# First products of a feed-forward by seven block products in place of eight

## The chip, the cores and the metric

The kernel runs on one core of a Trainium2 chip. Its time is the device time of one execution in microseconds (us); the figure for a kernel is the median of several executions. One execution of each kernel is also taken by the hardware profiler, and from that come the pages and rows shown here. TensorE is called PE there (PEld its weight load), VectorE DVE, ScalarE ACT, GpSimd POOL, and SyncE, which issues the loads, SP.

## The reference, cut to what matters

Two layers work on 512 latent tokens and, up to the end of the first layer, also on 256 context tokens. A layer is a half-step SwiGLU feed-forward, a mixer of four groups of heads, and a second feed-forward:

```python
def swiglu(h, w_in, w_out):
    u = h @ w_in                                    # 1024 x 5632
    return (jax.nn.silu(u[..., :D_FF]) * u[..., D_FF:]) @ w_out   # D_FF = 2816
...
x = x + 0.5 * mod[:, 2] * swiglu(modulate(rms_norm(x, norm_g[l, 0]), mod[:, 0], mod[:, 1]), ffn_w_in[l, 0], ffn_w_out[l, 0])
```

`modulate` scales and shifts each of the 1024 features; scale, shift and gate come from a product of a conditioning vector with `w_mod`, one set for the latent tokens and one for the context. The whole is in float32.

## The kernel before, in words

The stream xT lies in SBUF, features on partitions: eight tiles (KT) of 128 features by 768 tokens (T), the 512 latent tokens first and then the 256 of the context. Each weight and each activation of a large product is split in two fp32r parts, a high one (ScalarE rounds it) and a low one (VectorE subtracts; `split`, L371), and a product is three matmuls: high by high, high weight by low, low weight by high (`mm3`, L361). PE is given new weights for each matmul.

There are four feed-forward passes (`ffn`, L381): two in each layer. The last has the 512 latent tokens only. A pass runs over 22 blocks (`ff`) of 128 hidden features. For a block, the gate columns and the up columns of `ffn_w_in` are loaded as one raw tile of 128 x 2048 (w1r, L391), split as a whole, and multiplied over the eight feature tiles (u = 0 gate, u = 1 up) for both segments of tokens, 512 and 256 columns. Two more columns beside the second segment are the shifts of the modulation, so that their product gives the bias of the block (ub). The results in PSUM are scaled per token with the RMS norm (rsb) by VectorE (L419), ScalarE does SiLU, VectorE multiplies (L423), and the result is split again (gh, gl, L430 and L431). Blocks are gathered into chunks (CK, L1478); after the blocks of a chunk its second products run over the eight output tiles n_, and VectorE adds them to xT with the gate (L445). PSUM has seven banks for all of these.

In the background of the blocks, modulation vectors for later stages are made (`mod_block`, L201): tiles of `w_mod` of 1 MB are loaded and VectorE multiplies them by the conditioning vector and sums (macc, L213 and L215). Their instructions get a later place in the order (LATER).

Before a pass, `ready` (L335) is called after each finished tile of xT: it adds the tile's squares (`sumsq`) and makes its scaled high and low parts (`raw_tile`, L320) in hh and hlo. The last pass instead normalizes all tiles after the mixer (`norm_mod`, L344). The very first pass makes its own in a prologue (`first_mods`, L906), beside two modulation blocks on TensorE (`mod_direct`, L181).

The order on each engine is that of the program by these priorities, as a scheduler fixes it before the run; a dependence makes an engine wait, and then everything behind it on that engine waits. All loads are issued by SP, in order; a load waits until the tile that it overwrites is free.

## Time and profile before

| | |
|---|---|
| median of 3 runs | 3506.7 us (3506.53 to 3507.1) |
| the profiled execution | 3515.57 us, span 3513.8 us |
| PE busy | 3370.4 us, 96% of the span |
| DVE busy | 2001.4 us, 57% |
| ACT busy | 1144.4 us, 33% |
| POOL busy | 166.5 us, 5% |
| loaded from memory | 260.68 MB |

Busy time is the time in which an engine had an instruction at work; matmuls are pipelined and overlap, so a busy TensorE can still wait for short moments. The passes lie at 46 to 634, 1346 to 1943, 1943 to 2513 and 3100 to 3500 us of the span; the mixers lie between the first and the second and between the third and the fourth.

### The profile page before, as it was taken

The numbers are of one execution on the slowest core, as the hardware profiler recorded it, in microseconds if no ns is written. First come the engines' busy times: TensorE is split into PE (matmuls) and PEld (weight loads), VectorE is DVE, ScalarE is ACT, GpSimd is POOL, SyncE is SP. The second block draws the span as 40 slices with busy tenths as digits, with TensorE's granted clock in tenths as the row PEclk, the third lists the DMA queues.
The fourth block names the chain that finished last, engine by engine and source line by source line (L and its number), as shares of the span: only waits on it lengthen the run. The fifth ranks groups of instructions, "written<-read, shape, count | busy, mean of one in ns | idle before, by whom it ended". The sixth has DMA issues, their size and how long they took to land.

```text
span 3513.8 us, 54921 instructions
## 1 busy us (share of the span) xinstructions
PE 3370.4 (96%) x22756; PEld 2735.3 (78%) x22756; DVE 2001.4 (57%) x4351; ACT 1144.4 (33%) x2173; POOL 166.5 (5%) x350
## 2 busy tenths in 40 slices
PE   6999999999988999999999999999999989989997
PEld 5888888878666767888888788888888766667776
DVE  5776664555567856654445765443555568753333
ACT  3221122323456723211213112211333567532222
POOL 0000000000022310000000000000000022200000
PEclk8999999999999999999999999999999989999999
DMA  7444331211100014332121443331212100043330
GB/s 236 126 132 132 108 102 53 59 37 49 31 3 2 12 34 142 104 108 72 61 61 54 139 143 98 95 120 37 64 49 55 31 3 11 26 123 102 92 100 24
DMA packets 324121, 266.33 MB, mean 76 GB/s; under 512 B 27396, under 2 KB 273312, under 8 KB 323872
## 3 DMA queue, kind: packets, MB, share of 16 engines
q1 hardware_dynamic: 323872, 262.82, 24.5%
q8 instruction: 179, 2.93, 0.4%
q14 instruction: 70, 0.57, 0.1%
HBM read 260.68 MB, written 2.10 MB: 75 GB/s over the span
## 4 chain that ended last, share of the span: by engine, by line
PE 84%; DVE 10%; ACT 3%; issue 1%; DMA 1%; POOL 1%; DVEq 0%; SPq 0%; ACTq 0%; POOLq 0%
PE ul L365 13%; PE ul L367 13%; PE ul L369 13%; PE y L369 6%; PE y L367 6%; PE y L365 6%; PE pj L365 4%; PE pj L369 4%; PE pj L367 4%; PE op L1273 3%; PE S L1018 1%; PE ch L782 1%; DVE w1l L378 1%; PE gram L653 1%; PE po L1018 1%
## 5 line engine op out<-in xcount | busy, mean ns | idle before, releaser
L365 PE MATMUL ul<-hh,w1h 128*128 128x512 f32 (+1 forms) x2464 | 692.9, 350 | 2.5 <-ACT hh L357 1.6
L367 PE MATMUL ul<-hl,w1h 128*128 128x512 f32 (+1 forms) x2464 | 693.3, 348 | 1.5 <-DVE hl L358 1.5
L369 PE MATMUL ul<-hh,w1l 128*128 128x512 f32 (+1 forms) x2464 | 688.5, 348 | 1.5 <-DVE w1l L378 1.5
L365 PEld LDWEIGHTS ul<-hh,w1h 128*128 128x128 f32 x2464 | 395.9, 190 | 76.3 <-issue 9.9
L367 PEld LDWEIGHTS ul<-hl,w1h 128*128 128x128 f32 x2464 | 396.6, 190 | 66.4 <-DVE hl L358 2.2
L369 PEld LDWEIGHTS ul<-hh,w1l 128*128 128x128 f32 x2464 | 393.6, 189 | 63.9 <-DVE w1l L378 2.3
L367 PE MATMUL y<-gl,w2h 128*128 128x512 f32 x1232 | 342.8, 347 | 4.4 <-DVE gl L431 4.1
L369 PE MATMUL y<-gh,w2l 128*128 128x512 f32 x1232 | 339.0, 346 | 5.7 <-DVE w2l L378 5.7
L365 PE MATMUL y<-gh,w2h 128*128 128x512 f32 (+1 forms) x1232 | 340.1, 347 | 0.6 <-ACT gh L430 0.4
L377 ACT ACTIVATE w1h<-w1r 128x2048 fp32r<-128x2048 f32 x88 | 168.7, 1917 | 490.0 <-PE ul L367 454.1
L215 DVE SCALAR_TENSOR_TENSOR macc<-wm,sc,macc 128x512 f32<-128x512 f32 x392 | 274.2, 745 | 76.6 <-DMA wm<-in_w_mod_dram 75.2
L445 DVE SCALAR_TENSOR_TENSOR xT<-y,gate,xT 128x512 f32<-128x512 f32 x336 | 199.2, 631 | 192.3 <-PE y L369 191.7
L377 ACT ACTIVATE w2h<-wo 128x512 fp32r<-128x512 f32 (+1 forms) x192 | 111.6, 594 | 544.5 <-PE y L367 340.1
L365 PE MATMUL pj<-hh,pwh 128*128 128x512 f32 (+2 forms) x864 | 251.1, 342 | 3.9 <-DVE qA L945 1.8
L369 PE MATMUL pj<-hh,pwl 128*128 128x512 f32 (+2 forms) x864 | 243.0, 336 | 2.4 <-DVE pwl L378 2.4
L419 DVE TENSOR_TENSOR u<-ul,rsb 128x512 f32<-128x512 f32 (+1 forms) x132 | 70.8, 551 | 304.2 <-PE ul L369 304.2
L367 PE MATMUL pj<-hl,pwh 128*128 128x512 f32 (+2 forms) x864 | 242.9, 336 | 0.0
L369 PEld LDWEIGHTS y<-gh,w2l 128*128 128x128 f32 x1232 | 194.8, 188 | 40.0 <-DVE w2l L378 9.9
L367 PEld LDWEIGHTS y<-gl,w2h 128*128 128x128 f32 x1232 | 195.3, 188 | 38.3 <-DVE gl L431 8.9
L365 PEld LDWEIGHTS y<-gh,w2h 128*128 128x128 f32 x1232 | 195.4, 188 | 37.2 <-ACT w2h L377 3.1
L378 DVE TENSOR_TENSOR w1l<-w1r,w1h 128x2048 fp32r<-128x2048 f32 x88 | 201.2, 2286 | 26.6 <-ACT w1h L377 26.6
L421 ACT ACTIVATE sg<-sg,ub 128x512 f32<-128x512 f32 (+1 forms) x132 | 74.1, 609 | 425.7 <-DVE ub L416 321.0
(355 smaller groups left out, 4489.5 us busy)
## 6 DMA issues: line engine op xcount, KB each, us to landing
w1r<-in_ffn_w_in_dram SPq DMA_DIRECT2D x176, 512.0 KB
wm<-in_w_mod_dram SPq DMA_DIRECT2D x72, 1024.0 KB
wo<-in_ffn_w_out_dram SPq DMA_DIRECT2D x88, 512.0 KB
pw<-in_w_in_dram SPq DMA_DIRECT2D x46, 512.0 KB
pw<-in_w_in_dram SPq DMA_DIRECT2D x16, 256.0 KB
wo<-in_w_out_dram SPq DMA_DIRECT2D x128, 32.0 KB
wo<-in_w_out_dram SPq DMA_DIRECT2D x64, 64.0 KB
xl<-in_x_dram SPq DMA_DIRECT2D x4, 512.0 KB
```

The costliest lines, as they stand in the source:

```text
L215: nc.vector.scalar_tensor_tensor(out=acc[v], in0=r[:, k, :], scalar=s, in1=acc[v], op0=ALU.mult, op1=ALU.add)
L365: nc.tensor.matmul(p, lhsT=wh, rhs=xh[:, o:o + n], start=first, stop=False)
L367: nc.tensor.matmul(p, lhsT=wh, rhs=xl[:, o:o + n], start=False, stop=False)
L369: nc.tensor.matmul(p, lhsT=wl, rhs=xh[:, o:o + n], start=False, stop=last)
L377: nc.scalar.activation(out=hi, in_=raw, func=AF.Copy)
L378: nc.vector.tensor_tensor(out=lo, in0=raw, in1=hi, op=ALU.subtract)
L419: nc.vector.tensor_tensor(out=dst[:, o:o + n], in0=p, in1=self.rsb[:, o:o + n], op=ALU.mult)
L421: nc.scalar.activation(out=dst[:, o:o + n], in_=dst[:, o:o + n], func=AF.Silu, bias=b[:, u, s:s + 1])
L445: nc.vector.scalar_tensor_tensor(out=xs, in0=py[s], scalar=gt[s][:, n_:n_ + 1], in1=xs, op0=ALU.mult, op1=ALU.add)
L653: nc.tensor.matmul(pt[:, c, w], lhsT=BK[:, c, :], rhs=AR[:, e, c, w], start=True, stop=True)
L1018: mm = lambda out, lt, r, st, sp: nc.tensor.matmul(out, lhsT=lt, rhs=r, start=st, stop=sp, skip_group_check=True)
L1273: nc.tensor.matmul(p, lhsT=wt[:, i, :], rhs=os[i][:, osegs[i][v][0]:osegs[i][v][0] + c], start=i == 0, stop=i == m - 1)
```

## The change

The gate and up columns of a block, the even and the odd feature tiles, and the first and the second half of the tokens (H: 384 of 768, or 256 of 512) make a product of 2 x 2 by 2 x 2 blocks. It is done with seven block products in place of eight. `w1_operands` loads the four blocks of weights as tiles of 128 x 512 and makes four sums of them on GpSimd; each of the seven operands is split by itself, with four buffers for the parts. `up` issues the seven products, each 12 matmuls over 4 tiles, into three PSUM banks (b, c, a); ScalarE copies three partial results out, VectorE adds them to later ones, and results are also gathered in PSUM. The operands of the activations, B[0..6], are made for pairs of tiles when xT becomes ready (`pair_even`, `pair_odd`), two of the sums on GpSimd; the shift columns go with the four operands of SHIFTED.

Then the scaling by rsb is done by VectorE for one quarter of the results and by GpSimd for three. `up` of the next block, also across the end of a chunk, is issued behind the evaluation of a block and before the chunk's second products. The chunks become eight of two and three blocks. Tiles of `w_mod` are now 256 KB with two buffers, in the background and in the prologue, and the sums macc have one buffer each. The prologue loads the first block's weights once more to make its bias (bias0). `norm_mod` is gone; the last pass is prepared by `ready` as the others are. Before and after the feed-forwards that a mixer follows or precedes, the tiles hh and hlo and the tiles B take each other's place (`switch`).

```diff
+NWQ, NW1, NPC = 6, 4, 4
+MODPOOL = 0
+EVEN1, T1, T2, ODD1, T3, ODD2, T4 = range(7)
+SHIFTED = (EVEN1, T2, ODD1, T4)
...
+        acc = [self.fw.tile([128, 512], F32, name=f"macc{v}", tag=f"macc{v}", bufs=1) for v in vs]
+        for k in range(KT):
+            r = self.raw.tile([128, 512], F32, name="wm", tag="wm", bufs=2)
+            nc.sync.dma_start(out=r, in_=a["w_mod"][l, k * 128:(k + 1) * 128, b * 128:b * 128 + 512])
+                if k == 0:
+                    eng.tensor_scalar(out=acc[v], in0=r, scalar1=s, scalar2=None, op0=ALU.mult)
+                else:
+                    eng.scalar_tensor_tensor(out=acc[v], in0=r, scalar=s, in1=acc[v], op0=ALU.mult, op1=ALU.add)
         self.macc = l, b, vs, acc
...
+    def parts(self, i, m, x, scale=None):
+        nc = self.nc
+        hi, lo = (t[:, m, 2:] if i in SHIFTED else t[:, m, :] for t in self.B[i])
+        if scale is None:
+            nc.scalar.activation(out=hi, in_=x, func=AF.Copy)
+            nc.vector.tensor_tensor(out=lo, in0=x, in1=hi, op=ALU.subtract)
+        else:
+            nc.scalar.activation(out=hi, in_=x, func=AF.Copy, scale=scale)
+            nc.vector.scalar_tensor_tensor(out=lo, in0=x, scalar=scale, in1=hi, op0=ALU.mult, op1=ALU.subtract)
+    def second(self, k, segs, out):
+        H = self.half
+        for v, (o, n) in enumerate(segs):
+            o0, o1 = max(o, H), o + n
+            if o0 < o1:
+                self.nc.scalar.activation(out=out[:, o0 - H:o1 - H], in_=self.xT[k][:, o0:o1], func=AF.Copy, scale=self.rg[v][:, k:k + 1])
+    def pair_even(self, m, segs, e2):
+        k = 2 * m
+        self.parts(EVEN1, m, self.xT[k][:, :self.half], self.rg[0][:, k:k + 1])
+        self.second(k, segs, e2)
+    def pair_odd(self, m, segs, e2, o2, new):
+        nc, H = self.nc, self.half
+        e, o = self.xT[2 * m][:, :H], self.xT[2 * m + 1][:, :H]
+        ne, go = self.rg[-1][:, 2 * m:2 * m + 1], self.rg[0][:, 2 * m + 1:2 * m + 2]
+        self.second(2 * m + 1, segs, o2)
+        yield
+        t = new()
+        nc.vector.scalar_tensor_tensor(out=t, in0=e, scalar=ne, in1=e2, op0=ALU.mult, op1=ALU.add)
+        self.parts(T1, m, t)
+        yield
+        nc.gpsimd.tensor_tensor(out=t, in0=o2, in1=t, op=ALU.subtract)
+        self.parts(T2, m, t)
+        yield
+        self.parts(ODD1, m, o, go)
+        nc.gpsimd.tensor_tensor(out=e2, in0=o2, in1=e2, op=ALU.subtract)
+        self.parts(T3, m, e2)
+        yield
+        self.parts(ODD2, m, o2)
+        nc.vector.scalar_tensor_tensor(out=t, in0=o, scalar=go, in1=t, op0=ALU.mult, op1=ALU.subtract)
+        self.parts(T4, m, t)
+        yield
...
+            if n == 1:
+                self.raw_tile(k)
+                return
+            new = lambda tag="pc", bufs=NPC: self.tmp.tile([128, self.half], F32, name="x2", tag=tag, bufs=bufs)
+            if k % 2 == 0:
+                self.e2 = new("sg", 1)
+                self.pair_even(k // 2, segs, self.e2)
+            else:
+                for _ in self.pair_odd(k // 2, segs, self.e2, new(), new):
+                    pass
...
+    def w1_operands(self, l, i, ff):
+        nc = self.nc
+        new = lambda nm: self.raw.tile([128, KT // 2, 128], F32, name=nm, tag="wq", bufs=NWQ)
+        q = {}
+        for u, e in ((0, 0), (1, 0), (1, 1), (0, 1)):
+            q[u, e] = new("w1r")
+            c = (1 - u) * DFF + ff * 128
+            nc.sync.dma_start(out=q[u, e], in_=self.a["ffn_w_in"][l, i, :, c:c + 128].rearrange("(m e p) n -> e p m n", e=2, p=128)[e])
+        s = new("w1s")
+        cut = lambda t: self.split(t, [128, KT // 2, 128], "w1", bufs=NW1)
+        tt = lambda out, x, y, op: nc.gpsimd.tensor_tensor(out=out, in0=x, in1=y, op=op)
+        yield cut(q[0, 0])
+        tt(s, q[1, 0], q[1, 1], ALU.add)
+        yield cut(s)
+        tt(q[1, 0], q[0, 0], q[1, 0], ALU.subtract)
+        tt(q[0, 0], s, q[0, 0], ALU.subtract)
+        yield cut(q[0, 0])
+        yield cut(q[0, 1])
+        tt(q[0, 1], q[0, 1], q[0, 0], ALU.subtract)
+        yield cut(q[1, 0])
+        yield cut(q[0, 1])
+        yield cut(q[1, 1])
+    def up(self, l, i, ff, first):
+        nc, H = self.nc, self.half
+        W = H + 2
+        b, c, a = [self.psum("ul", "u") for _ in range(3)]
+        ops = self.w1_operands(l, i, ff)
+        z = 2 if first else 0
+        keep = lambda: self.fw.tile([128, W], F32, name="pc", tag="pc", bufs=NPC)
+        def product(n, out, start):
+            wh, wl = next(ops)
+            xh, xl = self.B[n]
+            x0 = z if n in SHIFTED else 0
+            for m in range(KT // 2):
+                for j, (w, x) in enumerate(((wh, xh), (wh, xl), (wl, xh))):
+                    nc.tensor.matmul(out, lhsT=w[:, m, :], rhs=x[:, m, x0:], start=start and m == j == 0, stop=m == KT // 2 - 1 and j == 2,
+                                     skip_group_check=True)
+        t = self.work.tile([128, 2 * H + 2], F32, name="u2", tag="t3")
+        g = self.fw.tile([128, 2 * H], F32, name="sg", tag="sg", bufs=1)
+        add = lambda out, x, y: nc.vector.tensor_tensor(out=out, in0=x, in1=y, op=ALU.add)
+        product(EVEN1, b[:, z:W], True)
+        p1 = keep()
+        nc.scalar.copy(p1[:, z:W], b[:, z:W])
+        product(T1, c[:, :H], True)
+        p5 = keep()
+        nc.scalar.copy(p5[:, :H], c[:, :H])
+        product(T2, b[:, z:W], False)
+        u2 = keep()
+        nc.scalar.copy(u2[:, :H], b[:, 2:W])
+        product(ODD1, a[:, z:W], True)
+        add(t[:, z:W], a[:, z:W], p1[:, z:W])
+        product(T3, b[:, 2:W], False)
+        add(g[:, H:], b[:, 2:W], p5[:, :H])
+        product(ODD2, c[:, :H], False)
+        add(t[:, W:], c[:, :H], u2[:, :H])
+        product(T4, b[:, z:W], False)
+        return t, g, b
...
             wo = self.raw.tile([128, cn, D], F32, name="wo", tag="wo", bufs=1)
             for j in range(cn):
                 ff = f + j
-                r = self.raw.tile([128, KT, 2, 128], F32, name="w1r", tag="raw", bufs=2)
-                for u in range(2):
-                    nc.sync.dma_start(out=r[:, :, u, :], in_=w1[l, i, :, u * DFF + ff * 128:u * DFF + (ff + 1) * 128].rearrange("(k p) n -> p k n", p=128))
+                first = l == i == ff == 0
+                if ff == 0:
+                    ahead = self.up(l, i, 0, first)
+                    if not first:
+                        self.raw_rows(self.fw, segs)
+                t, g, p = ahead
                 nc.sync.dma_start(out=wo[:, j, :], in_=w2[l, i, ff * 128:(ff + 1) * 128, :])
-                wh, wl = self.split(r, [128, KT, 2, 128], "w1")
-                us = []
...
-                for ss in ((0,), (1,)) if l == i == ff == 0 else (range(nseg),):
-                    for u in range(2):
-                        outs = [self.psum("ul", "u")[:, :cols[q][1]] for q in ss]
-                        for k in range(KT):
-                            self.mm3(outs, wh[:, k, u, :], wl[:, k, u, :], self.hh[:, k], self.hlo[:, k], [cols[q] for q in ss], k == 0, k == KT - 1)
-                        if ss[0] == 0:
...
+                n1 = 2 * H
+                mul = lambda eng, out, x, y: eng.tensor_tensor(out=out, in0=x, in1=y, op=ALU.mult)
+                mul(nc.vector, g[:, :H], p[:, 2:H + 2], self.rsb[:, :H])
+                mul(nc.gpsimd, g[:, H:], g[:, H:], self.rsb[:, H:])
+                mul(nc.gpsimd, t[:, 2:], t[:, 2:], self.rsb)
+                if first:
+                    b = self.bias0
                 else:
-                    nc.scalar.activation(out=g, in_=us[0][0], func=AF.Silu)
-                    nc.vector.tensor_tensor(out=g, in0=g, in1=us[1][0], op=ALU.mult)
+                    b = self.fw.tile([128, 2, 2], F32, name="ub", tag="ub", bufs=2)
+                    nc.vector.tensor_copy(b[:, 0, :], t[:, 0:2])
+                    nc.vector.tensor_copy(b[:, 1, :], p[:, 0:2])
+                for s, (o, n) in enumerate(segs):
+                    nc.scalar.activation(out=g[:, o:o + n], in_=g[:, o:o + n], func=AF.Silu, bias=b[:, 1, s:s + 1])
+                for s, (o, n) in enumerate(segs):
+                    nc.vector.scalar_tensor_tensor(out=g[:, o:o + n], in0=t[:, 2 + o:2 + o + n], scalar=b[:, 0, s:s + 1], in1=g[:, o:o + n],
+                                                   op0=ALU.add, op1=ALU.mult)
...
                 self.mod_sum()
                 with self.tc.high_priority(offset=-LATER):
                     background(ff)
+                if ff < DFF // 128 - 1:
+                    ahead = self.up(l, i, ff + 1, False)
             if ci == 0:
                 gt = self.gates(l, 2 * i, segs, 0.5)
+            if ci == len(chunks) - 1 and switch:
+                switch()
             for n_ in range(KT):
...
+    def pairs_open(self, n=T):
+        self.hx = ExitStack()
+        p = self.pool(self.hx, "hp", 1, side="right")
+        self.half = n // 2
+        self.B = [[p.tile([128, KT // 2, self.half + (2 if i in SHIFTED else 0)], F32R, name=f"b{q}{i}") for q in "hl"] for i in range(7)]
...
+            self.mod_direct(0, b, ring(self.hl, "w1h", 4, NW1) + ring(self.hl, "w1l", 4, NW1))
+        halves = []
+        for m in range(KT // 2):
+            x2 = self.hl.tile([128, 2, self.half], F32, name="x2", tag=("gh", "gl")[m % 2], bufs=3)
+            halves.append((x2[:, 0, :], x2[:, 1, :]))
+            self.pair_even(m, SEGS, halves[m][0])
+        new = lambda: self.fw.tile([128, self.half], F32, name="x2", tag="pc", bufs=NPC)
+        stages = [self.pair_odd(m, SEGS, *halves[m], new) for m in range(KT // 2)]
+        for _ in range(5):
+            for s in stages:
+                next(s)
...
-            w = self.raw.tile([128, 8, 512], F32, name="wm8", tag="wo", bufs=1)
-            self.mod_direct(0, 0, [lambda i=i: w[:, 4 * i:4 * i + 4, :] for i in range(2)])
-            self.mod_direct(0, 4, (buf(self.raw, "wm", 1), buf(self.raw, "raw", 2)))
+            for b in (0, 4):
+                w = self.raw.tile([128, 6, 512], F32, name="wm6", tag="wo", bufs=1)
+                self.mod_direct(0, b, [w[:, i, :] for i in range(6)] + ring(self.raw, "wm", 2, 2))
+            w = self.raw.tile([128, KT, 256], F32, name="wb", tag="wo", bufs=1)
+            for u in range(2):
+                nc.sync.dma_start(out=w[:, :, 128 * u:128 * u + 128],
+                                  in_=self.a["ffn_w_in"][0, 0, :, (1 - u) * DFF:(1 - u) * DFF + 128].rearrange("(k p) n -> p k n", p=128))
...
+                gx.close()
+                self.pairs_open(segs[-1][0] + segs[-1][1])
+                self.tmp = self.wop = self.pool(rx, "wop", 4)
...
-        CK = [3, 3, 4, 4, 4, 4]
+        CK = [3, 2, 2, 3, 3, 3, 3, 3]
...
-        self.ff(0, 0, SEGS, CK, bg[0], self.ready(0, 1), True)
+        def switch():
+            self.hx.close()
+            self.h_open()
+        self.ff(0, 0, SEGS, CK, bg[0], self.ready(0, 1), True, switch)
-        self.ff(1, 0, SEGS, CK, bg[2], self.ready(1, 1))
-        self.mixer(1, lambda k: self.sumsq(k, SEGS[:1]))
+        self.ff(1, 0, SEGS, CK, bg[2], self.ready(1, 1), switch=switch)
+        self.mixer(1, self.ready(1, 2, SEGS[:1]))
         self.ff(1, 1, SEGS[:1], CK, bg[3], None)
```

## Rows read from the trace of the kernel before

**Rows 1.** Busy time by stage; columns: stretch, length, engines (instructions), granted clock, DMA, GB/s
```profile
46.00:634.00 588.00, 586.63 (x3395) 500.55 (x3395) 377.18 (x654) 133.11 (x179) 1.41 (x2) 1.00 0.36 111
...
1346.00:1943.00 597.00, 590.61 (x3359) 511.55 (x3360) 310.16 (x528) 136.76 (x176) 0.22 (x2) 0.99 0.29 88
1943.00:2513.00 570.00, 562.87 (x3206) 484.40 (x3205) 310.07 (x534) 126.16 (x169) 1.02 (x2) 0.99 0.31 97
...
3100.00:3500.00 400.00, 382.54 (x1628) 301.42 (x1628) 158.53 (x197) 109.31 (x137) 0.00 (x0) 0.98 0.29 87
```

**Rows 2.** Waits of TensorE in the second products: total us, times, longest
```profile
PE y L369 <- DVE w2l L378: 5.7, 10, 0.9
```

**Rows 3.** Timeline of TensorE, three stretches: start, us, line, tiles, form, count
```profile
1394.72 0.51 PE L365 MATMUL ul<-hh,w1h 128*128 128x512 f32 x2
...
1407.07 0.53 PE L369 MATMUL ul<-hh,w1l 128*128 128x512 f32 x2
...
3170.14 0.39 PE L369 MATMUL ul<-hh,w1l 128*128 128x512 f32 x1
...
3173.87 0.39 PE L365 MATMUL ul<-hh,w1h 128*128 128x512 f32 x1
...
2540.34 0.40 PE L365 MATMUL pj<-hh,pwh 128*128 128x256 f32 x2
...
2541.30 0.40 PE L367 MATMUL pj<-hl,pwh 128*128 128x256 f32 x2
```

**Rows 4.** Groups of VectorE's instructions by form: count, busy us, mean ns, idle before
```profile
L378 DVE TENSOR_TENSOR w1l<-w1r,w1h 128x2048 fp32r<-128x2048 f32 x88 | 201.2, 2286 | 26.6 <-ACT w1h L377 26.6
...
L445 DVE SCALAR_TENSOR_TENSOR xT<-y,gate,xT 128x512 f32<-128x512 f32 x192 | 143.4, 749 | 192.3 <-PE y L369 191.7
...
L378 DVE TENSOR_TENSOR w2l<-wo,w2h 128x512 fp32r<-128x512 f32 x128 | 85.8, 683 | 36.6 <-ACT w2h L377 36.6
...
L445 DVE SCALAR_TENSOR_TENSOR xT<-y,gate,xT 128x256 f32<-128x256 f32 x144 | 68.3, 475 | 0.0
...
L419 DVE TENSOR_TENSOR sg<-ul,rsb 128x512 f32<-128x512 f32 x66 | 45.4, 688 | 149.9 <-PE ul L369 149.9
...
L378 DVE TENSOR_TENSOR w2l<-wo,w2h 128x384 fp32r<-128x384 f32 x64 | 34.1, 549 | 7.5 <-ACT w2h L377 7.5
...
L419 DVE TENSOR_TENSOR u<-ul,rsb 128x256 f32<-128x256 f32 x66 | 27.3, 414 | 0.0
...
L416 DVE COPY ub<-ul 128x2 f32<-128x2 f32 x132 | 19.9, 151 | 19.5 <-PE ul L369 19.0
```

**Rows 5.** Timeline of VectorE: four modulation sums that follow each other
```profile
306.45 2.73 DVE L215 SCALAR_TENSOR_TENSOR macc<-wm,sc,macc 128x512 f32<-128x512 f32 x4
```

**Rows 6.** Groups of GpSimd's instructions by form
```profile
L640 POOL TENSOR_TENSOR AR<-zr,pp 64x256 f32<-64x256 f32 x40 | 28.8, 720 | 21.8 <-ACT pp L606 19.0
L527 POOL TENSOR_TENSOR zv<-zv,zt 128x128 f32<-128x128 f32 x48 | 23.6, 492 | 11.9 <-ACT zv L521 8.5
```

**Rows 7.** Timeline of the first mixer, then two lines' durations: min/median/max ns
```profile
1024.88 0.75 DVE L641 SCALAR_TENSOR_TENSOR kk<-ra,kk 128x256 f32<-128x256 f32 x1
1024.90 0.45 POOL L527 TENSOR_TENSOR zr<-zr,zt 128x128 f32<-128x128 f32 x1
...
1025.99 1.49 POOL L640 TENSOR_TENSOR AR<-zr,pp 64x256 f32<-64x256 f32 x2
1026.12 0.83 DVE L645 TENSOR_TENSOR BK<-kk,su 128x256 f32<-128x256 f32 x1
1026.87 0.89 DVE L641 SCALAR_TENSOR_TENSOR kk<-ra,kk 128x256 f32<-128x256 f32 x1
...
L645 DVE TENSOR_TENSOR BK<-kk,su x24: 401/419/827, 1026.1 to 3027.0; 128x256 f32<-128x256 f32 x24
...
L641 DVE SCALAR_TENSOR_TENSOR kk<-ra,kk x24: 408/416/893, 1024.9 to 3024.5; 128x256 f32<-128x256 f32 x24
```

**Rows 8.** Who waited for the modulation tiles: us, times
```profile
DVE macc L215: 75.2, 24
```

More of the change, by code (lines that the diff above doesn't have):

```diff
@@ L906, in first_mods @@
     def first_mods(self):
[L908 to L910 removed]
+        nc = self.nc
+        ring = lambda pool, tag, n, bufs: [pool.tile([128, 512], F32, name="wm", tag=tag, bufs=bufs) for _ in range(n)]
         for b in (8, 12):
[L912 to L913 removed]
+            self.mod_direct(0, b, ring(self.hl, "w1h", 4, NW1) + ring(self.hl, "w1l", 4, NW1))
```

159 lines of the change are left out of this document (65 added, 94 removed).

## The prediction

> **What bounds the kernel now.** I read the busy time by stage first, then the waits, then the timeline. [rows 1] are the four feed-forward passes (layer 0 first, layer 0 second, layer 1 first, layer 1 second: passes 0 to 3 below), 588, 597, 570 and 400 us. In each of them TensorE is busy 96% of the time or more, while VectorE is busy 377, 310, 310 and 159 us. So the passes are paced by the matmul stream, and everything else lies under it. The waits say the same: what TensorE waits for inside the second products, the largest entry being the low part of their weights, is 5.7 us in the whole run [rows 2]. Two things follow. Fewer columns through TensorE is worth its full price as long as the other engines stay under it. And issuing the next chunk's first products between the last chunk's work can win little by itself in passes 0 to 2, because there is hardly a hole to fill.
>
> **The price of a matmul** comes from the distance between starts, since the shown durations overlap [rows 3]. In passes 0 to 2 the first products go in pairs of 512 and 258 columns: from 1394.72 to 1407.07 lie 35 pairs, 0.353 us each. In pass 3, with 512 columns alone, 16 matmuls take 3.73 us, 0.233 each. Matmuls of 256 columns in the second mixer, which have the same new weights for each: eight in 0.96 us, 0.120 each. So the weight load is not the limit down to 256 columns.
>
> **What TensorE loses.** Per block of 128 hidden columns (22 to a pass) the kernel now issues 48 pairs, 16.94 us. The change issues 7 products x 4 tiles x 3 = 84 matmuls of 384 or 386 columns. Half a pair is 385 columns, so each is 0.1765 us: 14.83 us. That saves 2.11 us a block, 46.5 us a pass, in passes 0 to 2. In pass 3, 48 x 0.233 = 11.19 us become 84 x 0.1205 (256 or 258 columns) = 10.12 us: 1.07 a block, 23.5 us. In all 163 us. The second products keep their matmuls; they are only cut into eight chunks in place of six. Were nothing else in the way, the passes would be 541.5, 550.5, 523.5 and 376.5 us.
>
> **What VectorE gains in work** [rows 4]. Instructions that follow each other directly cost less than their shown duration: four modulation sums of 512 columns take 2.73, 0.68 each [rows 5], where one such operation by itself shows 0.749 (the xT row). I take 0.08 off each. Removed per block in passes 0 to 2: one low split of 2048 columns (2.286) and two scalings of 512 + 256 from PSUM (2 x (0.688 + 0.414)): 4.09 net. Added: seven low splits of 512 (7 x 0.683), and three sums and one scaling of 384 from PSUM, which lie between the 256 and the 512 row, 0.551 each: 6.11 net. That is +2.0 a block, +44 a pass. Two more chunks give 16 more updates of xT, each 0.749 + 0.475: +17 a pass. The splits of w2 change by +1. The operands built for pass 2 at the end of pass 1 (per pair of tiles nine instructions of about 0.55 in place of four like the xT rows) add 8. VectorE then has 440, 381 and 372 us in passes 0 to 2. In pass 3 one split and one scaling go (2.82 net), and seven splits, four PSUM operations of 256, two small copies and a 512-wide final product come (6.36 net): +78, and +12 for chunks and w2, 249 us. So by its own work VectorE stays below TensorE everywhere, but in pass 0 at 81% where it was 64%. ScalarE, now busy 133 us of pass 0 [rows 1], gets about 5 us a block more and stays under half.
>
> **What GpSimd gets.** It is idle in the passes now. Per block it gets four sums of 512 columns and scalings of 384 and 768. Its two-input operations took 492 ns for 128 columns and 720 ns for 256 [rows 6], 1.78 ns a column: 1.18, 0.95 and 1.63 us, 7.3 us a block, 160 us a pass (6.6 and 145 in pass 3). By itself that hides. But it does not run beside VectorE freely. Three VectorE operations with two SBUF inputs, each 0.42 us as a rule, took 0.75, 0.83 and 0.89 us while GpSimd's sums ran (0.45 us, then two in 1.49), and each of them ended about a quarter microsecond behind the end of a GpSimd operation [rows 7]. They lost 1.22 us to 1.94 us of GpSimd: a share of 0.63. Most of VectorE's work in the passes is of that kind (the splits, the products in SBUF, the modulation sums macc); sums from PSUM are not.
> The Trainium skill, SBUF — State Buffer, section "Who interferes with whom", speaks against this change here: a VectorE instruction with two SBUF inputs and a GpSimd instruction that reads SBUF exclude each other for the whole instruction. The trace agrees in kind, with its share of 0.63; by the page, with nothing else for VectorE to do, the share would be 1, the case of the second rival. The same skill's GPSIMD Engine Reference, section "Performance versus the Vector engine", gives 4497 ns for 2048 columns; by it, an estimate, a block would have 7.0 us on GpSimd.
>
> With 0.63 of GpSimd's time on top VectorE has 541, 482, 473 and 340 us. The bounds are 440, 381, 372, 249 (share 0) and 600, 541, 532, 394 (share 1). I take 0.63, since VectorE was busy without a gap where it was measured, as it would be here.
>
> **Other edits.** The modulation weights come in tiles of 256 KB with two buffers instead of 1 MB with one. VectorE stands in order behind each, and with it the splits that TensorE waits for. Now such waits are 75.2 us in 24 times [rows 8], about 3 each, and they are hidden because VectorE has time. In pass 0, with 14 blocks of modulation, VectorE no longer has it, so I add 14 x 3 = 42 us there: 583. Bounds 0 and twice that.
> In passes 1 to 3 TensorE still ends last, but VectorE is at 88 to 90% of its time and in order. Each next product needs a fresh split, and T4 needs the sum g[:, H:] out of its bank within the one product (2.1 us) that stands between. I take 0.5 us a block lost, 11 a pass; bounds 0 and one product, 2.1.
> The prologue builds 56 split operands before the first products and loads 1 MB more for bias0: +10 (0 to 20). At the end of the first mixer the tail is already VectorE's: +9. At the end of pass 1 the +8 of the operands is on the path too. In pass 3 the wait for the next chunk's whole split at each of five boundaries goes, since the products ahead are split in pieces: −12 (0 to −20).
> The loads on SP keep their bytes and become smaller: four of 256 KB a block for w1r in place of two of 512, in a ring of six tiles with the sum s, and eight in place of two for a block of modulation. The queues are loaded to 29 to 36% in the passes [rows 1]. But SP issues in order: a modulation tile waits for two macc operations, and the w1r tiles behind it wait too, so a late VectorE makes loads late and these make splits late. That loop is inside the 42 and the 11 us; it has no price of its own in the rows.
> More chunks cost TensorE nothing: the updates of xT run under the next matmuls, and cost 17 us a pass only where VectorE is the bound, which is counted.
>
> **The sum**, against the profiled span of 3513.8 us: pass 0 −5 (583 for 588), pass 1 −35.5, pass 2 −27 (46.5 less 11 and 8), pass 3 −24.5, prologue +10, mixer tail +9: −73, a span of 3441. The median of the timed runs, 3506.7, is 7.1 below the profiled span, so I forecast 3434 us.
>
> **Rivals.** (1) GpSimd costs VectorE nothing that counts: VectorE has slack in every pass, no product waits, and the whole 163 us comes less prologue, mixer tail and operands (27), with 12 from pass 3: −148, 3359 us. For it: the share was measured in a short stretch, and sums of weights may fall where VectorE reads PSUM. Against it: pass 0 has no room.
> (2) The other sign: GpSimd and VectorE exclude each other fully, share 1. Passes 0 to 3 are then VectorE's: 600 + 42, 541 + 18, 532 + 36 (six and twelve blocks of modulation) and 394 + 10, so +54, −38, −2 and +4; with prologue, tail and operands +45: 3552 us. From share 0.63 to 1 the sum rises by 118, so it turns slower at about 0.86. For it: the operations in [rows 7] ended with GpSimd's. Against it: a fourth of VectorE's time reads PSUM.
> (3) The reordering does nothing and TensorE does not get shorter per block, because 84 matmuls of 384 columns each wait for their weight loads: the time stays within 7 us. Against it: 256 columns at 0.120 us [rows 3].
>
> **Chances.** The forecast's mechanism 0.43 (own range 3395 to 3490), rival 1 0.27, rival 2 0.25, rival 3 0.05. A measurement tells 0.2%, 7 us, from no change. Faster 0.70, within 0.2% 0.05, slower 0.25. The range of 3345 to 3555 takes in both outer cases.
>
> **What would show it.** The steps of first products at 0.1765 us, and their sum per block near 14.8 us. GpSimd near 160 us a pass, and low splits whose mean is well over 0.683: about 0.15 to 0.3 us more means share 0.63; the macc sums too. Pass 0 hardly shorter than 588 while passes 1 to 3 lose 25 to 36 each. TensorE's waits should name the low splits and the sums g and t, which now do not appear. The forecast is wrong if those means do not move (rival 1), if TensorE is idle by several microseconds in every block also in passes 1 and 2 (rival 2), or if the order of the loads stops SP's queue and TensorE waits for w1r.

## The result, and the profile after

The changed kernel takes 3643.5 us (3636.2 to 3650.3) against 3506.9 us for the kernel before: a ratio of 1.0386, 95% interval [1.0365, 1.0408]. It is 3.9% slower; 3434 us, 2.1% faster, was predicted, and even the slower rival's 3552 us lies below it. The profiled execution has a span of 3634.4 us, 120.6 more than before.

The stages, each from the first `ul` matmul of a pass to the first `pj` matmul of the mixer behind it, or back; in us of the span (mixer 0 includes what is made for the pass behind it):

| | ahead | pass 0 | mixer 0 | passes 1 and 2 | mixer 1 | pass 3 to end |
|---|---|---|---|---|---|---|
| before | 52.0 | 583.2 | 714.2 | 1165.6 | 592.4 | 406.4 |
| after | 56.0 | 649.9 | 724.9 | 1170.1 | 597.2 | 436.3 |
| difference | +4.0 | +66.7 | +10.7 | +4.5 | +4.8 | +29.9 |

The engines' line of the page, after:

```profile
PE 3304.8 (91%) x22788; PEld 2804.5 (77%) x22788; DVE 2680.1 (74%) x5306; ACT 1496.4 (41%) x3168; POOL 1010.8 (28%) x910
```

TensorE is busy for less time than before, 3305 for 3370 us, and yet the run is longer: it idles. Busy time of the four passes after (columns as in [rows 1]):

```profile
56.00:705.90 649.90, 580.85 (x3136) 518.73 (x3135) 564.79 (x859) 215.81 (x409) 213.55 (x132) 0.95 0.35 105
1430.80:2005.00 574.20, 537.97 (x2990) 500.46 (x2990) 441.32 (x706) 219.03 (x411) 217.97 (x138) 0.98 0.27 83
2005.00:2600.90 595.90, 556.77 (x3039) 510.48 (x3039) 473.18 (x741) 213.83 (x397) 208.02 (x137) 0.96 0.34 100
3198.10:3634.00 435.90, 372.98 (x2425) 335.93 (x2425) 325.60 (x497) 179.42 (x348) 172.53 (x134) 0.95 0.26 80
```

Where [rows 1] show TensorE at 96% or more, it is at 86 to 94% here; VectorE is at 75 to 87%. No engine is full, so the passes are set by engines that wait for each other. The granted clock of TensorE is 0.95 to 0.98 where it was 0.98 to 1.00. One place at the end of pass 2 shows what that is (start, us; x2 is a pair):

```profile
2592.22 0.51 PE L428 MATMUL y<-gh,w2h 128*128 128x512 f32 x2
2592.57 0.51 PE L430 MATMUL y<-gl,w2h 128*128 128x512 f32 x2
2596.55 0.92 PE L432 MATMUL y<-gh,w2l 128*128 128x512 f32 x2 [3.48 <-DVE w2l L441]
2597.27 0.84 PE L428 MATMUL y<-gh,w2h 128*128 128x512 f32 x2
2597.91 0.84 PE L430 MATMUL y<-gl,w2h 128*128 128x512 f32 x2
```

TensorE waits 3.48 us for a low split of w2, and behind the wait its pairs start 0.64 us apart where they were 0.35 apart. The granted clock is 1.00 from 2585 to 2593 us and 0.55 from 2596.5 to 2600.3: for most of that stretch the lower of its two levels, 1.2 GHz in place of 2.4.

TensorE's waits, which before had nothing over 6 us in the second products [rows 2] (columns: waiting instruction, whose work ended the wait; total us, times, longest):

```profile
PE ul L484 <- DVE sg L489: 66.0, 35, 3.7
PE y L432 <- DVE w2l L441: 37.3, 25, 4.1
PE ul L484 <- ACT pc L492: 36.0, 28, 3.0
PE modps L242 <- DVE macc L227: 23.0, 11, 3.9
```

The first is of a product that may not enter its PSUM bank before VectorE has read the sum for g out of it. VectorE's and GpSimd's forms after, and between them VectorE's modulation sum before:

```profile
L441 DVE TENSOR_TENSOR w1l<-w1r,w1h 128x512 fp32r<-128x512 f32 x528 | 441.3, 839 | 82.6 <-ACT w1h L440 81.7
L227 DVE SCALAR_TENSOR_TENSOR macc<-wm,sc,macc 128x512 f32<-128x512 f32 x392 | 414.2, 1076 | 7.0 <-DMA wm<-in_w_mod_dram 6.6
L563 DVE SCALAR_TENSOR_TENSOR xT<-y,gate,xT 128x512 f32<-128x512 f32 x256 | 191.1, 747 | 167.2 <-PE y L432 166.8
...
L489 DVE TENSOR_TENSOR u<-ul,pc 128x384 f32<-128x384 f32 x67 | 36.8, 549 | 19.5 <-PE ul L484 19.5
```
```profile
L215 DVE SCALAR_TENSOR_TENSOR macc<-wm,sc,macc 128x512 f32<-128x512 f32 x392 | 274.2, 745 | 76.6 <-DMA wm<-in_w_mod_dram 75.2
```
```profile
L455 POOL TENSOR_TENSOR w1r<-w1r 128x512 f32<-128x512 f32 x176 | 269.8, 1533 | 164.9 <-issue 108.1 <-POOL u L526 25.4 <-ACT pc L495 15.6
...
L526 POOL TENSOR_TENSOR u<-u,rsb 128x768 f32<-128x768 f32 x66 | 127.0, 1924 | 61.9 <-DVE u L489 61.9
L526 POOL TENSOR_TENSOR sg<-sg,rsb 128x384 f32<-128x384 f32 x66 | 93.2, 1412 | 59.0 <-DVE sg L489 56.8 <-ACT rsb L404 0.4
```

The split of 512 columns takes 0.839 us where [rows 4] have 0.683, the modulation sum 1.076 where it took 0.745. The update of xT (0.747, 0.749 before) and the sum u from PSUM (0.549; 0.554 in a run below in which GpSimd is idle) have not moved: of their inputs one lies in PSUM and one in SBUF. The timeline of GpSimd and VectorE in pass 1 shows how it happens (start, us):

```profile
1654.06 2.44 DVE L227 SCALAR_TENSOR_TENSOR macc<-wm,sc,macc 128x512 f32<-128x512 f32 x2
1654.22 1.73 POOL L455 TENSOR_TENSOR w1s<-w1r 128x512 f32<-128x512 f32 x1 [4.55 <-DVE w1l L441]
...
1656.03 1.63 POOL L455 TENSOR_TENSOR w1r<-w1r 128x512 f32<-128x512 f32 x1
1656.42 1.78 DVE L441 TENSOR_TENSOR w1l<-w1r,w1h 128x512 fp32r<-128x512 f32 x1
1658.13 0.74 DVE L227 SCALAR_TENSOR_TENSOR macc<-wm,sc,macc 128x512 f32<-128x512 f32 x1
```

GpSimd's sums end at 1655.95 and 1657.66; VectorE's operations that started beside them end at 1656.50 and 1658.20, 0.55 us behind each, as if they had waited out the whole sum and then run. The next one, with GpSimd idle, takes 0.74. The whole trace says the same: of the 616 splits of weight blocks 125 begin while a sum of GpSimd runs, and the middle half of these ends 0.546 to 0.549 us behind that sum; the other 491 take 0.68 us in the median.

### The profile page after: what moved, and what is told of

Same layout as the page of the kernel before. It is cut to its first block, busy times and chain, and to the rows that moved or that the text cites. A ratio compares the mean times of both kernels' runs of the same rounds, so it can differ in the third digit from the quotient of the medians.

```text
span 3634.4 us, 59477 instructions
## 1 busy us (share of the span) xinstructions
PE 3304.8 (91%) x22788; PEld 2804.5 (77%) x22788; DVE 2680.1 (74%) x5306; ACT 1496.4 (41%) x3168; POOL 1010.8 (28%) x910
## 5 line engine op out<-in xcount | busy, mean ns | idle before, releaser
L484 PE MATMUL ul<-bh,w1h 128*128 128x386 f32 (+3 forms) x2464 | 833.3, 338 | 115.0 <-DVE sg L489 66.0
L484 PE MATMUL ul<-bh,w1l 128*128 128x386 f32 (+3 forms) x2464 | 816.9, 332 | 1.1 <-DVE w1l L441 1.0
L484 PE MATMUL ul<-bl,w1h 128*128 128x386 f32 (+3 forms) x2464 | 816.3, 331 | 0.0
L484 PEld LDWEIGHTS ul<-bh,w1h 128*128 128x128 f32 x2464 | 478.9, 194 | 157.8 <-DVE sg L489 72.0
L440 ACT ACTIVATE w1h<-w1r 128x512 fp32r<-128x512 f32 x528 | 329.9, 631 | 546.2 <-PE ul L484 311.0
L441 DVE TENSOR_TENSOR w1l<-w1r,w1h 128x512 fp32r<-128x512 f32 x528 | 441.3, 839 | 82.6 <-ACT w1h L440 81.7
L484 PEld LDWEIGHTS ul<-bh,w1l 128*128 128x128 f32 x2464 | 477.9, 194 | 9.7 <-issue 6.9
L484 PEld LDWEIGHTS ul<-bl,w1h 128*128 128x128 f32 x2464 | 479.7, 195 | 3.1 <-issue 2.9
L428 PE MATMUL y<-gh,w2h 128*128 128x512 f32 x1232 | 351.5, 355 | 13.0 <-ACT w2h L440 10.9
L455 POOL TENSOR_TENSOR w1r<-w1r 128x512 f32<-128x512 f32 x176 | 269.8, 1533 | 164.9 <-issue 108.1
```

What stands on the lines that cost most here:

```text
L428: nc.tensor.matmul(p, lhsT=wh, rhs=xh[:, o:o + n], start=first, stop=False)
L440: nc.scalar.activation(out=hi, in_=raw, func=AF.Copy)
L441: nc.vector.tensor_tensor(out=lo, in0=raw, in1=hi, op=ALU.subtract)
L455: tt = lambda out, x, y, op: nc.gpsimd.tensor_tensor(out=out, in0=x, in1=y, op=op)
L484: nc.tensor.matmul(out, lhsT=w[:, m, :], rhs=x[:, m, x0:], start=start and m == j == 0, stop=m == KT // 2 - 1 and j == 2, skip_group_check ...
```

## The experiments

The theory (X where the expectations give it a letter) is that GpSimd's operations hold VectorE out, and the late VectorE stops TensorE. The rival is that GpSimd is itself late, and that the splits, which wait for its sums, stop TensorE. Other suspects: the products and their order, the chunks, the modulation tiles. Beside each group of experiments the kernel before was timed again, at 3511 to 3523 us, and differences from it are taken within the group; a difference between kernels of two groups, the 149 and 46 below among them, is uncertain by some 10 us more. A ratio has its 95% interval; a time without a ratio is that of one execution. Four executions of one kernel lay 5 to 24 us apart, so a difference of a few us is none.

**The sums on VectorE.**

```diff
-        tt = lambda out, x, y, op: nc.gpsimd.tensor_tensor(out=out, in0=x, in1=y, op=op)
+        tt = lambda out, x, y, op: nc.vector.tensor_tensor(out=out, in0=x, in1=y, op=op)
```

> The kernel after, with the four sums of weights on VectorE; the two scalings stay on GpSimd. Theory X (GpSimd and VectorE hold each other out for whole instructions, which makes VectorE the bound in pass 0 and late everywhere): low splits of w1 fall from 0.84 to about 0.70 us in the mean, macc sums from 1.08 to about 0.85; VectorE gets 2.4 us a block more of its own, but the whole gets shorter, a span of 3450 to 3560. Theory R (the seven products with their chain of banks and small splits stall TensorE whoever makes the sums): VectorE has more to do and the span is 3634 or more.

Measured: 3494.1 us, ratio 0.9933 [0.9909, 0.9958], as theory X has it; the low splits take 0.713 us and the modulation sums 0.908. The same sums cost 149 us more on GpSimd than on VectorE.

**The scalings too**, in addition to the sums:

```diff
-                mul(nc.gpsimd, g[:, H:], g[:, H:], self.rsb[:, H:])
-                mul(nc.gpsimd, t[:, 2:], t[:, 2:], self.rsb)
+                mul(nc.vector, g[:, H:], g[:, H:], self.rsb[:, H:])
+                mul(nc.vector, t[:, 2:], t[:, 2:], self.rsb)
```

> The kernel after, with the sums of weights and the two scalings on VectorE: GpSimd does nothing in the passes. Theory X: low splits at 0.68 and macc at 0.75 as before the change, VectorE near 520 us by its own work in pass 0, span 3420 to 3550, clock back near 0.98. Theory R: span 3634 or more.

Measured: 3448.4 us, ratio 0.9814 [0.9795, 0.9832]. VectorE's forms of this kernel are back at their lengths:

```profile
L441 DVE TENSOR_TENSOR w1l<-w1r,w1h 128x512 fp32r<-128x512 f32 x528 | 357.3, 687 | 44.8 <-ACT w1h L440 43.1 <-PE ul L484 0.3
L227 DVE SCALAR_TENSOR_TENSOR macc<-wm,sc,macc 128x512 f32<-128x512 f32 x392 | 283.6, 747 | 7.0 <-DMA wm<-in_w_mod_dram 6.4
```

and its windows (pass 0; passes 1 and 2; pass 3):

```profile
58.00:634.00 576.00, 558.40 (x3135) 509.86 (x3135) 530.32 (x986) 216.58 (x406) 1.77 (x3) 0.98 0.40 118
1364.00:2463.00 1099.00, 1074.45 (x6029) 1001.13 (x6029) 933.86 (x1708) 434.87 (x808) 14.01 (x13) 0.98 0.32 98
3059.00:3442.00 383.00, 356.77 (x2427) 326.47 (x2427) 321.72 (x631) 177.76 (x348) 1.07 (x4) 0.97 0.29 89
```

VectorE is busy for 92% of pass 0, a larger share than after the change (87%), and the pass is 74 us shorter. So a full VectorE was not what made the changed kernel slow.

**No sums at all.**

```diff
-        tt(s, q[1, 0], q[1, 1], ALU.add)
-        yield cut(s)
...
+        for k in ((0, 0), (1, 1), (0, 0), (0, 1), (1, 0), (0, 1)):
+            yield cut(q[k])
```

> As the run before it, and the four sums of weights are left out: the seven splits take the raw blocks, so the seven products are no longer those of the reference. Theory X: VectorE has 2.4 us a block less than in the run before, nothing waits for sums, and the structure itself shows its gain: span 3360 to 3440. Theory R: the chain of banks and small splits still stalls, 3550 or more.

Measured: 3400.2 us, span 3398.4; pass 0 takes 559 us, passes 1 and 2 together 1092, pass 3 371. This is what the seven products give when nobody pays for the sums of weights.

**Scalings on VectorE, sums on GpSimd** (the scalings' edit alone).

> The kernel after, with the two scalings on VectorE; the four sums of weights stay on GpSimd. This is the other half of the change that the run with the sums on VectorE undid. Theory X, in a form in which what GpSimd does simply adds up: the scalings on GpSimd cost 52 us (3494 against 3442 in the two runs' spans), so the span is 3634 less 52, about 3580. If lateness of the sums is the larger part, it is 3560 or more; if the two scalings had blocked most, below 3520.

Measured: 3597.1 us (span 3595), 46 below the changed kernel. With the second experiment the sums cost 149 again. The span lies near the 3580 of theory X, but also above the 3560 named for late sums, so this run alone does not tell the two apart; the next one does.

**Idle sums**: as the last, with the sums of GpSimd written to a tile that nobody reads.

```diff
-        yield cut(s)
-        tt(q[1, 0], q[0, 0], q[1, 0], ALU.subtract)
-        tt(q[0, 0], s, q[0, 0], ALU.subtract)
+        yield cut(q[1, 1])
+        tt(s, q[0, 0], q[1, 0], ALU.subtract)
+        tt(s, q[1, 1], q[0, 0], ALU.subtract)
```

> As the run with the scalings on VectorE, but the seven splits take raw blocks and the four sums on GpSimd are written to a tile that nobody reads (the products are not those of the reference). VectorE's and GpSimd's work is that of the run before it; only nobody waits for a sum. Reference points: 3398 us without any sums; about 3580 with sums in use. If holding out by itself is what costs (theory X), the span is within 50 us of the run with the sums in use. If it is the wait for the sums (theory L, lateness: sums of 1.5 us stand in the chain of the splits), the span is within 50 us of 3398.

Measured: 3617.5 us. No split waits for a sum any more, and the time doesn't fall: the wait of the splits for late sums is out as the cause. What a late GpSimd still does here is hold the weight tiles that it reads; a later experiment takes that away too.

**Memsets in place of the idle sums**, three for each, so that GpSimd is as busy but reads nothing:

```diff
+            for _ in range(3):
+                nc.gpsimd.memset(out, 0.0)
```

> As the run with sums that nobody reads, but each of the four sums on GpSimd is replaced by three memsets of the same tile, which write SBUF and read nothing (splits of raw blocks, so the products are not those of the reference). GpSimd's busy time stays of the same order, about 100 to 140 us a pass. If it is the reading that holds VectorE out, as the Trainium skill has it (SBUF — State Buffer, Who interferes with whom), the span is near the 3398 us without sums, within 30. If any activity of GpSimd does it, the span is over 3520.

Measured: 3406.2 us, within 6 of the kernel without sums. The windows of pass 0, first with idle sums, then with memsets:

```profile
55.00:685.00 630.00, 571.99 (x3137) 520.28 (x3137) 560.60 (x908) 220.29 (x412) 139.61 (x87) 0.96 0.36 108
```
```profile
55.00:613.00 558.00, 549.02 (x3134) 505.22 (x3134) 488.25 (x907) 218.23 (x405) 135.88 (x255) 0.99 0.40 122
```

and the low splits of these two kernels over the whole run:

```profile
L441 DVE TENSOR_TENSOR w1l<-w1r,w1h 128x512 fp32r<-128x512 f32 x616 | 536.0, 873 | 78.9 <-ACT w1h L440 77.6
L441 DVE TENSOR_TENSOR w1l<-w1r,w1h 128x512 fp32r<-128x512 f32 x616 | 423.2, 689 | 81.0 <-ACT w1h L440 77.4 <-DMA wm<-in_w_mod_dram 0.6
```

GpSimd is busy for 140 and 136 us, and VectorE, with the same work, for 561 and 488. The Trainium skill, SBUF — State Buffer, section "Who interferes with whom", says that a VectorE instruction with two SBUF inputs contends with a GpSimd instruction that reads SBUF, and not with one that only writes it. The traces agree: a split takes 0.873 us beside the sums and 0.689 beside the memsets.

**Idle sums of one fixed tile**, since idle sums also hold the weight tiles from being loaded anew:

```diff
-        tt = lambda out, x, y, op: nc.gpsimd.tensor_tensor(out=out, in0=x, in1=y, op=op)
+        r = self.ident.rearrange("p (o n) -> p o n", o=1).to_broadcast([128, KT // 2, 128])
+        tt = lambda out, x, y, op: nc.gpsimd.tensor_tensor(out=out, in0=r, in1=r, op=op)
```

> As the idle sums (3617 us), but GpSimd's sums read one fixed tile and write the same spare tile, so no weight tile is held for them. Output is not the reference's, since raw blocks take the place of the sums. Theory X, the reading shuts VectorE out: within 40 us of 3617, and low splits well over 0.69 us. Theory R, the raw tiles held by GpSimd made the loads and so the splits late: 3406 to 3450 us, as with the memsets.

Measured: 3544.2 us, 138 above the memsets and 73 below the idle sums, so between the times that the two theories named. The low splits stay long:

```profile
L441 DVE TENSOR_TENSOR w1l<-w1r,w1h 128x512 fp32r<-128x512 f32 x616 | 498.5, 812 | 70.5 <-ACT w1h L440 67.3 <-PE modps L203 0.5
```

The reading alone makes about two thirds of the loss. The last third goes with the held tiles and with GpSimd's time, which is also less here (1.33 us a sum for 1.57); these two are not told apart.

**ScalarE reads the bank** that TensorE waits for, in the kernel with idle sums and in the one with scalings on VectorE:

```diff
-        add(g[:, H:], b[:, 2:W], p5[:, :H])
+        p6 = keep()
+        nc.scalar.copy(p6[:, :H], b[:, 2:W])
+        add(g[:, H:], p6[:, :H], p5[:, :H])
```

> The kernel with the idle sums on GpSimd (3617 us, sums that nobody reads), with one edit: ScalarE copies the result of T3 out of its bank, and VectorE adds it to the earlier copy from there, so that T4 waits for ScalarE and not for VectorE. Output is not the reference's, since raw blocks take the place of the sums. Theory P, the place: TensorE's 102 us of waiting for g are what the late VectorE costs first; they go, and the clock recovers: 3500 to 3550 us. Theory Q, VectorE as a whole is late: the wait turns up at the splits or at the other sums: 3590 us or more.

> The changed kernel with its scalings on VectorE (3597 us) and ScalarE's copy of T3's result, nothing left out. Theory P: 3500 to 3545 us; TensorE's 65 us of waiting for g are gone. Theory Q: 3575 us or more.

Measured: 3614.5 and 3603.0 us, as without the copy (3617.5 and 3597.1). Theory P falls. The wait goes from VectorE to ScalarE and to the second products, as TensorE's waits of the idle sums without and with the copy show:

```profile
PE ul L484 <- DVE sg L489: 101.6, 45, 3.6
```
```profile
PE ul L484 <- ACT pc L492: 63.5, 31, 3.3
PE y L432 <- DVE w2l L441: 37.6, 28, 4.1
PE modps L242 <- DVE macc L227: 25.3, 14, 6.6
```

L492 is not the new copy but that of the block's first result, for which TensorE waited 13.5 us without the edit; for w2l it waited 24.3 us. So it is not one dependence that fails: taken away in one place, the wait comes out in others, as theory Q has it. The new copy also takes a fourth of the four buffers for copies in each block; what that costs beside a busy GpSimd no run separates, beside an idle one it is nothing clear (the last experiment).

**GpSimd's sums in the kernel before**: four sums a block in the raw tile, behind the reading by its splits.

```diff
+                for u in range(2):
+                    for h in range(2):
+                        nc.gpsimd.tensor_tensor(out=r[:, 4 * h:4 * h + 4, u, :], in0=r[:, :4, u, :], in1=r[:, 4:, u, :], op=ALU.add)
```

> The kernel before, with four sums of 512 columns a block on GpSimd, made in place in the raw weight tile behind its splits; their results go nowhere, so the output is unchanged. Theory X: the means of VectorE's two-input operations rise as in the kernel after (macc from 0.745 to about 1.0, w1l by some tenths), GpSimd's sums take about 1.5 us, VectorE's busy time grows by some 150 us, and the time grows little (3510 to 3570), since VectorE had room. Theory R: means unchanged, sums at 1.2 us, time 3507.

Measured: 3623.2 us, 109 above the kernel before, though it has neither the products nor the chunks of the change, and more than the 3570 at which theory X ended. Its modulation sums take 0.969 us for 0.745 and its VectorE is busy for 152 us more in the passes, as expected; its splits of w1, which the sums stand behind, hardly move (2.311 for 2.286). It too holds the weight tile longer, so the 109 are not the exclusion alone. That VectorE had room (busy for 377 of 588 us in pass 0 before [rows 1], 433 of 625 here) did not keep the time from growing.

**The order alone**: the kernel before with the next block's first products issued ahead, across chunks too; `up(ff + 1)` is called behind the split of a block's result.

> The kernel before, with eight block products as they were, and only the next block's first products issued ahead, behind the evaluation of a block and before the second products. By the prediction's reading there is hardly a hole to fill in passes 0 to 2, and some 13 us in pass 3: span 3490 to 3514.

Measured: 3497.8 us, 17 below the kernel before, ratio 0.9948 [0.9931, 0.9965].

**The small edits**: the kernel before with eight chunks and modulation tiles of 256 KB; then the chunks alone; then the chunks with the products ahead.

```diff
-        CK = [3, 3, 4, 4, 4, 4]
+        CK = [3, 2, 2, 3, 3, 3, 3, 3]
```

> The kernel before, with the eight chunks of two and three blocks and with modulation tiles of 256 KB in two buffers, and nothing else. By the prediction these edits cost nothing while VectorE has room: 3505 to 3525 us. If the small tiles make VectorE wait in order (the prediction's 42 us in pass 0), pass 0 grows by 20 us or more.

> The kernel before with one edit: eight chunks of two and three blocks in place of six of three and four. The two small edits together (chunks and 256 KB modulation tiles) came out 61 us above the kernel before. Theory A, the chunks: at each boundary of a chunk TensorE has nothing to do until the last block's scaling, SiLU, product and split are done; two more boundaries a pass, eight in all, at 5 to 8 us each: 40 to 64 us above the kernel before. Theory B, the tiles: VectorE and with it the splits stand behind a late small tile; then the chunks alone are within 12 us of the kernel before.

> The kernel before with the next block's first products issued ahead (its own time was 3498 us, 0.9948 of the kernel before) and with the eight chunks. Theory A, the chunks cost what they cost because TensorE has nothing to do at a boundary: with the products ahead it has, so the time is within 10 us of 3498. Theory C, each chunk costs its updates of xT and its own start whatever is issued ahead: 25 us or more above 3498.

Measured: 3584.1, 3583.5 and 3532.4 us. The first was a miss: 61 us above the kernel before, not nothing. The chunks alone cost 67, so no cost of the small tiles shows here. With the products ahead the chunks still cost 35 (3532.4 for 3497.8), which is theory C's figure and not theory A's: issuing ahead takes away about half of what the chunks cost, as theory A would have it for all, and the other half stays. Why it stays was not tried. TensorE's waits with the chunks alone:

```profile
PE y L367 <- DVE gl L431: 20.7, 17, 2.1
...
PE y L369 <- DVE w2l L378: 18.0, 22, 3.2
```

where before they were 4.1 us for gl and 5.7 us for w2l [rows 2]. With fewer blocks in a chunk TensorE asks for the next split of w2 sooner. With the products ahead the wait for gl falls to 0.2 us, and 13.7 us for w2l stay.

**A better version**: sums and scalings on VectorE, and two modulation blocks each moved from pass 0 to pass 1 and from pass 2 to pass 3; then the same with ScalarE's copy.

```diff
-        bg = [blocks(t) for t in (cols(0, 16, 72), cols(1, 0, 24), cols(1, 24, 72), [])]
+        bg = [blocks(cols(0, 16, 64)), early(cols(0, 64, 72), cols(1, 0, 24)), blocks(cols(1, 24, 64)), early(cols(1, 64, 72), [])]
```

> The run with all on VectorE, and two of the 14 modulation blocks of pass 0 moved to the start of pass 1, two of the 12 of pass 2 to the start of pass 3. Pass 0 took 576 us there against 559 without sums of weights, so VectorE still sets part of its pace; each block is about 11 us of VectorE: pass 0 shorter by 5 to 20, passes 1 and 2 unchanged, pass 3 longer by 0 to 8. Span 3420 to 3442.

> The best kernel so far (all sums and scalings on VectorE, four modulation blocks moved to later passes, 3440 us, 0.9784 of the kernel before) with ScalarE's copy of T3's result. Where GpSimd is idle TensorE hardly waits for g, so by theory P there is little to gain: 3425 to 3445 us. By Q too. What would surprise: over 20 us either way.

Measured: 3440.0 us, ratio 0.9784 [0.9765, 0.9802], and 3444.7, 0.9818 [0.9785, 0.9851], both as expected; the copy gains nothing. The first beats both kernels: 2.2% below the one before.

## Why the prediction was wrong

**The bound and the price of a matmul: right.** "Each is 0.1765 us": the first products of the changed kernel start 0.17 to 0.18 us apart, as its timeline shows:

```profile
57.68 0.33 PE L484 MATMUL ul<-bh,w1h 128*128 128x384 f32 x1
57.85 0.34 PE L484 MATMUL ul<-bl,w1h 128*128 128x384 f32 x1
58.03 0.34 PE L484 MATMUL ul<-bh,w1l 128*128 128x384 f32 x1
```

Most of the gain of 163 us is there: without the sums of weights TensorE is busy for 1970 us in the passes, against 2115 before, 145 less. The span of that run is 115 below before. An account that takes the forecast's −163 and adds what runs measured, the order −17, the chunks with that order +35, prologue and mixers +17 (55.7, 721.3 and 598.9 us of that kernel against 52.0, 714.2 and 592.4), comes to −128 and leaves 13 for all else, VectorE's added splits among it. Rival 3 is out.

**VectorE's load: right in the sum, and not what decides.** Predicted with the share of 0.63 were 541, 482, 473 and 340 us, 1836 in all; measured 565, 441, 473 and 326, 1805 in all. That it was right in the sum is luck, for both factors of GpSimd's part were off, and in opposite directions: 1.53 us a sum for 1.18, 812 us in the passes for 625, and a smaller share. Idle sums against memsets give that share by itself: VectorE 1858 and 1609 us over the passes, GpSimd 553: 0.45 for 0.63. So 365 us (812 x 0.45) stand where 394 (625 x 0.63) were put. The 0.63 came from three operations in a stretch in which VectorE had no gap [rows 7].

**The step that failed** is the one behind it: "In passes 1 to 3 TensorE still ends last ... I take 0.5 us a block lost, 11 a pass; bounds 0 and one product, 2.1", and in pass 0 VectorE's sum as the length of the pass. It took the pass to be as long as its fullest engine and put little on the engines' waiting for each other. The passes are longer than either engine's time. Of the 193 us between the forecast span of 3441 and the measured one, 72 lie in pass 0, 67 in passes 1 and 2, and 54 in pass 3. Against the stages before less the saving that was forecast (536.7, 1072.6 and 370.9 us, the last also less the 12 at its boundaries) pass 0, passes 1 and 2, and pass 3 are 113, 98 and 65 us longer: 5.1, 2.2 and 3.0 us in each of their blocks. In passes 1 and 2 that is the upper bound of the term (2.0 without the 8 us of operands, which the forecast booked by themselves); in pass 3 it is above it, and pass 0, for which no such term was put, has more than twice the bound.

In place of the term, the experiments show two prices. These are the sums of the passes for five kernels: no sums, sums on VectorE, memsets, idle sums, idle sums of one fixed tile (the scalings are on VectorE in all):

```profile
sum 2022.00, PE 1969.59 PEld 1828.30 DVE 1596.42 ACT 838.57 POOL 16.38; mean PE 656.53 PEld 609.43 DVE 532.14 ACT 279.52 POOL 5.46
sum 2058.00, PE 1989.62 PEld 1837.46 DVE 1785.90 ACT 829.21 POOL 16.84; mean PE 663.21 PEld 612.49 DVE 595.30 ACT 276.40 POOL 5.61
sum 2021.00, PE 1968.53 PEld 1827.90 DVE 1609.49 ACT 836.22 POOL 558.47; mean PE 656.18 PEld 609.30 DVE 536.50 ACT 278.74 POOL 186.16
sum 2236.00, PE 2038.21 PEld 1869.51 DVE 1857.92 ACT 835.38 POOL 553.14; mean PE 679.40 PEld 623.17 DVE 619.31 ACT 278.46 POOL 184.38
sum 2152.00, PE 2003.93 PEld 1840.18 DVE 1783.71 ACT 832.06 POOL 471.13; mean PE 667.98 PEld 613.39 DVE 594.57 ACT 277.35 POOL 157.04
```

VectorE's own work is cheap: the sums done on VectorE add 190 us to its busy time (1786 for 1596) and 36 to the passes (2058 for 2022). Waiting behind GpSimd is not: idle sums of one fixed tile in place of memsets add 174 us to VectorE's busy time (1784 for 1609) and 131 to the passes (2152 for 2021); idle sums that also hold weight tiles add 248 and 215. The second and the last of the five rows say it at once: VectorE is busy for the same time, 1786 and 1784 us, and the passes differ by 94. So VectorE's busy time does not set the length of a pass here. Of the 215, 70 are TensorE's busy time (2038 for 1969): with the idle sums the granted clock is lower (0.96, 0.97 and 0.94 for 0.99, 0.99 and 0.98 in pass 0, passes 1 and 2, and pass 3), and matmuls then take longer. The prediction left the clock out. The other 145 are waits. Why a microsecond of waiting costs so much more than one of work stays open: the held tiles make little of it (215 of 248 with them, 131 of 174 without), and the order in which GpSimd's sums and VectorE's splits fall in a block was not tried.

**Rival 2** had the sign and, for two operations that meet, the mechanism ("GpSimd and VectorE exclude each other fully"), but not its size: its share of 1 gives VectorE 600, 541, 532 and 394 us, 2067 in all, and 1805 were measured. Its time still came short by 91 us, since it too made each pass VectorE's busy time. Pass 0 came near (+67 for its +54), passes 1 and 2 far off (+4.5 for −40), pass 3 too (+30 for +4). TensorE's idle time, by which the prediction would have told rival 2, is 1.7 us a block in passes 1 and 2 and about 3 in passes 0 and 3. The outer bound of the range, 3555, rested on rival 2's sum, so the time fell out of it.

**The modulation tiles**: 42 us were put on pass 0; no cost of the small tiles shows by themselves. VectorE's waits for them [rows 8] are 6.6 us after, for 75.2 before and 70.9 in the kernel before with small tiles. **Chunks**: "More chunks cost TensorE nothing" was wrong: 35 us in the kernel before with the products ahead. **The order** in the kernel before gives 17 us. The 12 that stood for it in pass 3 are near that by luck, for it is spread: 2.5, 9.5 and 8 in pass 0, in passes 1 and 2, and in pass 3. **Prologue**, mixer tail: +4 and +10.7 for +10 and +9.

In sum: of the changed kernel's 3643 us, the sums on GpSimd in place of VectorE are 149 and the scalings 46; without these two choices the change gives 3448 us. That this is only 14 above the forecast does not bear it out: the forecast had put GpSimd's load and the small tiles into pass 0, and that kernel has no such load on GpSimd.

## What to carry to other kernels

An idle GpSimd is not free room beside a VectorE on whose two-input operations TensorE waits: ask first whether both read SBUF, and try the work on VectorE itself, even where it is then busy for 92% of a pass, as here. Do not take a pass to be as long as its fullest engine when engines wait for each other in short steps: here passes of equal VectorE busy time differed by 94 us in all. A forecast from busy shares needs the delay of a single operation on the chain beside it, and the clock that a stalling TensorE loses. Price "small" edits that come with a change, such as the cut into chunks, by a run of their own: here one of them cost 35 to 67 us.

## What the runs showed of the hardware

What GpSimd does counts, not how long it is busy: 558 us of memsets (0.529 us each) left VectorE's splits at 0.689 us, 469 us of sums of one fixed tile brought them to 0.812, and 553 us of sums of weights to 0.873. The exclusion works in both directions: of GpSimd's sums in the changed kernel the 98 that begin while VectorE is idle take 1.30 us in the mean, and the 220 that begin while a VectorE operation with two SBUF inputs is at work 1.68. The spread of one form of them (durations: least/median/most ns, first and last start):

```profile
L455 POOL TENSOR_TENSOR w1r<-w1r x176: 1267/1622/1965, 34.8 to 3582.4; 128x512 f32<-128x512 f32 x176
```

The granted clock goes with TensorE's stalls: it was 0.99 where TensorE idles 9 of 558 us (memsets, pass 0) and 0.96 where it idles 58 of 630 (idle sums, pass 0), and behind one wait of 3.48 us it was 0.55 for 3.8 us.
